# SBUF pools at multiples of 512 bytes, split weights 64 bytes into their tiles, in a hybrid decoder block

## The chip, the cores and the metric

One core of a Trainium2 chip runs the kernel. The metric is the device time of one execution in microseconds (us): the median of three timed executions before is 2871.86 (2871.25 to 2874.51). A further execution was recorded by the profiler. Engines are named as the profile names them: PE is TensorE, with PEld for its weight loads, DVE is VectorE, ACT is ScalarE, POOL is GpSimd, SP is SyncE, which issues the DMAs.

## The reference

One layer of a decoder block on a sequence of 512 tokens with 2,048 channels, all in float32: conditioning by `c`, an input projection, a gated short convolution and a gated linear recurrence (HGRN2) side by side, a merge, a SwiGLU network and three norms.

```python
def reference(x, c, w_ada, b_ada, norm_mix_g, w_in, conv_w, lb_param, gnorm_g,
              w_conv_out, w_hgrn_out, w_o, norm_ffn_g, w_ffn_gate, w_ffn_up, w_ffn_down,
              norm_final_g):
...
        h = rmsnorm(x, norm_mix_g[l]) * (1.0 + sc_m) + sh_m
        proj = h @ w_in[l]
        a_b, a_c, a_x, q, f_logit, i_in, g_out, gate_a, gate_b = jnp.split(proj, split_idx, axis=-1)

        y_a = (a_b * causal_depthwise_conv(a_c * a_x, conv_w[l])) @ w_conv_out[l]
...
        y_b = o.reshape(b, s, D_HGRN_V).astype(x.dtype) @ w_hgrn_out[l]

        merged = jax.nn.sigmoid(gate_a) * y_a + jax.nn.sigmoid(gate_b) * y_b
        x = x + gt_m * (merged @ w_o[l])

        h2 = rmsnorm(x, norm_ffn_g[l]) * (1.0 + sc_f) + sh_f
        ff = (jax.nn.silu(h2 @ w_ffn_gate[l]) * (h2 @ w_ffn_up[l])) @ w_ffn_down[l]
        x = x + gt_f * ff
```

## The kernel before

**Three products for one.** A float32 matrix product is made of three matmuls in the type float32r. Both operands are split: `hi` is the value rounded to float32r (a cast on ACT), `lo` is the rest (a subtraction on DVE). `mm3` (lines 218 to 225) and `m3` (618 to 621) issue weights-hi by activations-hi, weights-hi by activations-lo and weights-lo by activations-hi into one PSUM tile. Each matmul first loads a block of 128 x 128 weights, the stationary operand (LDWEIGHTS on PEld), and then streams the moving operand, 128 partitions by 256 or 512 columns of 4 bytes. The program has 17,316 float32r matmuls: 5,568 with 512 columns (lines 223 to 225, and 619 to 621 with a moving operand called hc) and 11,748 with 256 (all other of 619 to 621, some of 223 to 225, and lines 341 to 343). Plain float32 matmuls are few: 616, in the recurrence (lines 478 to 537) and in the sums of squares for the norms (289, 545, 918, 924), where a tile of ones is the weight.

**Operands change sides once.** In `v_block` (lines 334 to 343, 768 matmuls) the activations `h` are loaded as weights and the split weights `hi` and `lo` are the moving operand.

**Stages.** (1) 0 to 215 us: activations come in, the first modulation rows are reduced by DVE from 33.6 MB of `w_ada` (line 301), and the first projections run. (2) 215 to 772: the projections `q`, `f`, `g`, `v` and the convolution by `proj` and `v_block` with 512 columns, and the recurrence's small matmuls between them. (3) 772 to 1080: the gates, by one level of Strassen's scheme (`st_pass`, seven products of 256 columns in place of eight). (4) 1080 to 1390: the output projections with 512 columns, while DVE reduces the other modulation rows (`wm`, line 301), 67 MB of them over stages 2 and 4. (5) 1390 to 1465: the last of them with 256 columns. (6) 1465 to 2740: the SwiGLU network; Strassen passes for gate and up projections alternate with `down`, whose moving operand hc has 512 columns. (7) 2740 to 2868: the last down projection by halves of the tokens, the final norm, and the output.

**How weights arrive.** SP issues DMAs of 512 KB into `wr`, `ur` or `wm`. For each tile of weights ACT writes `hi` and DVE writes `lo`; in Strassen passes (`quad_s`, lines 663 to 670) DVE also forms four sums first. The pools of split weights are `wts` (stages 1 to 5, tiles of 4 x 256 or 8 x 128), `wts2` (stage 6, 7 x 128) and `tailw` (stage 7, 4 x 128). Weights are prepared two tiles ahead of their use (`next_w`, `next_g`, `next_u`). For two passes of stage 6 split weights are kept in the tiles `sb` of another pool (`kept`): 192 matmuls read them from there.

**Where tiles lie.** A pool is a range of each partition's SBUF bytes; pools are stacked from the left in the order in which they are opened, those with `side="right"` from the right end, and a pool opened later may stand where a closed one stood. In the built program of before, the first 16,384 bytes are scratch for DMA descriptors of software queues, small constants follow, and the pool `persist` lies from 16,512 to 22,496. From there on every pool on the left begins at 480 modulo 512, and so do the pools of activations on the right (`acto` at 196,576, `sacta` at 184,288), since tiles in them are multiples of 512 bytes. Slices of operands are steps of 512 or 1,024 bytes. So all 17,316 float32r matmuls have both weights and moving operand at 96 modulo 128 bytes. The tile of ones is at 0 modulo 128.

The order in which instructions stand on the engines is decided when the program is built, and is fixed then.

Of the kernel before, what the change touches and what calls it, by code (L numbers as in the profile page):

```python
# [8 lines left out]
F32 = mybir.dt.float32  # L9
F32R = mybir.dt.float32r  # L10
# [4 lines left out]
P = 128  # L15
# [26 lines left out]
RAMPS = (6,)  # L42
WFULL = 5
HCB = 5

COL_C = 0
COL_B = 16
# [14 lines left out]
def hybrid_block_kernel(ctx: ExitStack, tc: tile.TileContext, xt, cols, crow, wam, war, wst, win, wco, who, wo, wgt, wg, wu, wd,  # L62
                        cf, out):
    nc = tc.nc
    cnt = [0]

    def nm(s):
        cnt[0] += 1
        return f"{s}{cnt[0]}"

    pp = ctx.enter_context(tc.tile_pool(name="persist", bufs=1, reuse_waits="tile"))
    xpool = ctx.enter_context(tc.tile_pool(name="xact", bufs=8, reuse_waits="tile"))
    s1 = ctx.enter_context(ExitStack())
    r1 = ctx.enter_context(ExitStack())
# [6 lines left out]
    wp = s1.enter_context(tc.tile_pool(name="wts", bufs=3, reuse_waits="tile"))  # L81
# [35 lines left out]
    lbc = cp.tile([P, 64], F32, name="lbc")  # L117
    smat = cp.tile([P, 2, 4, P], F32, name="smat")
    epsc = pp.tile([P, 1], F32, name="epsc")
    ra = pp.tile([P, 2, T], F32, name="ra")  # L120
    rt = ra[:, 0, :]
    sums_ = {"t": ra[:, 1, :]}
# [8 lines left out]
    wlist = []  # L131
    wstate = {"dma": 0, "prep": 0, "use": 0, "raw": {}, "hl": {}}

    def w_pair(shape):
        return [wp.tile(list(shape), F32R, tag=t, name=nm(t)) for t in ("hi", "lo")]

    def w_dma():
        i = wstate["dma"]
# [8 lines left out]
    def w_prep():  # L147
        i = wstate["prep"]
        if i >= len(wlist):
            return  # L150
        while wstate["dma"] <= i:
            w_dma()
        raw = wstate["raw"].pop(i)
        hi, lo = w_pair((P, 4, 256))
        nw = wlist[i].shape[-1]
        S.copy(flat(hi)[:, 0:nw], raw[:, 0:nw])  # L156
        V.tensor_tensor(flat(lo)[:, 0:nw], raw[:, 0:nw], flat(hi)[:, 0:nw].bitcast(F32), op=ALU.subtract)  # L157
        wstate["hl"][i] = (hi, lo)
        wstate["prep"] = i + 1
# [503 lines left out]
    def quad_s(sm, raw, hi, lo):  # L663
        S.copy(hi[:, 0:3, :], raw[:, 1:4, :])  # L664
        V.tensor_tensor(sm[:, 0:2, :], raw[:, 1:3, :], raw[:, 0:1, :].to_broadcast([P, 2, P]), op=ALU.subtract)
        V.tensor_tensor(sm[:, 2, :], sm[:, 1, :], raw[:, 1, :], op=ALU.add)
        V.tensor_tensor(sm[:, 3, :], raw[:, 3, :], sm[:, 2, :], op=ALU.subtract)  # L667
        S.copy(hi[:, 3:7, :], sm)  # L668
        V.tensor_tensor(lo[:, 0:3, :], raw[:, 1:4, :], hi[:, 0:3, :].bitcast(F32), op=ALU.subtract)
        V.tensor_tensor(lo[:, 3:7, :], sm, hi[:, 3:7, :].bitcast(F32), op=ALU.subtract)  # L670
# [85 lines left out]
    def g_prep():  # L756
        i = gs["prep"]
        while gs["dma"] <= i:
            g_dma()
        _, _, u, strassen = glist[i]  # L760
        raw = gs["raw"].pop(i)[:, u, :, :]
        hi, lo = w_pair((P, 8, P))
        if strassen:
            quad_s(gs["sm"](), raw, hi, lo)
        else:
            quad_c(raw, hi, lo)
        gs["hl"][i] = (hi, lo)
        gs["prep"] = i + 1
# [196 lines left out]
    def u_dma():  # L965
        i = us["dma"]
        src = ulist[i][0] if i < tail0 else wd[(i - tail0) // 2, 10]
        raw = wr2.tile([P, 2, 4, P], F32, tag="raw", name=nm("ur"))
        nc.sync.dma_start(raw, src.rearrange("p (u b n) -> p u b n", u=2, b=4))
        if i < tail0:  # L970
            us["raw"][i] = us["raw"][i + 1] = raw
        else:
            for u in range(2):
                us["raw"][tail0 + torder.index(((i - tail0) // 2, u))] = raw
        us["dma"] = i + 2
# [64 lines left out]
    wp2 = s2.enter_context(tc.tile_pool(name="wts2", bufs=3, reuse_waits="tile"))  # L1040
    hcp = s2.enter_context(tc.tile_pool(name="hc", bufs=HCB, reuse_waits="tile"))
    tmp = s2.enter_context(tc.tile_pool(name="evt", bufs=1, reuse_waits="tile"))
# [10 lines left out]
    def u_prep():  # L1053
        i = us["prep"]
        while i not in us["raw"]:
            u_dma()
        _, u, kind = ulist[i]
        raw = us["raw"].pop(i)[:, u, :, :]
        pool = us["pool"] if kind == "T" else wp2
        shp = [P, 4, P] if kind == "T" else [P, 7, P]  # L1060
        if kind == "H":
            k = len(kept)
            t = sb[k // 2][k % 2]
            hi, lo = (t[:, 1 + 2 * b:3 + 2 * b, :].rearrange("p a (c n) -> p (a c) n", n=P) for b in range(2))
            kept.append((hi, lo))
        else:
            hi = pool.tile(shp, F32R, tag="hi", name=nm("uh"))
            lo = pool.tile(shp, F32R, tag="lo", name=nm("ul"))
        if kind == "S":
            quad_s(wp2.tile([P, 4, P], F32, tag="sm", name=nm("us"), bufs=2), raw, hi, lo)  # L1070
        else:
            with ExitStack() as order:
                for ins in us["after"] if i >= len(ulist) - 12 else ():
                    order.enter_context(tc.issue_after(ins.ins))
                S.copy(hi[:, 0:4, :], raw)  # L1075
                V.tensor_tensor(lo[:, 0:4, :], raw, hi[:, 0:4, :].bitcast(F32), op=ALU.subtract)  # L1076
        us["hl"][i] = (hi, lo)
        us["prep"] = i + 1

    def u_ahead(n=ULOOK):  # L1080
        i = us["use"]
        for k in range(i, min(i + n + 1, len(ulist))):
            if ulist[k][2] == "T" and us["pool"] is None:
                break
            if us["prep"] <= k:
                u_prep()
        while us["dma"] <= min(i + n + 3, len(ulist) - 2):
            u_dma()
# [305 lines left out]
```

## Time and profile before

| what | us |
|---|---|
| median of three timed executions | 2871.86 |
| the profiled execution's own time | 2870.43 |
| its span, first to last instruction | 2868.7 |
| PE busy | 2784.0 |
| DVE busy | 2237.1 |
| ACT busy | 1094.6 |

The span is what the profile covers; 1.7 us of the execution's time lie outside it. Busy time of PE counts a matmul from when it starts to wait for its columns to when its results are modelled to be out, so matmuls overlap in the records, and the distance of their starts tells more than their length. The mean granted TensorE clock is 0.992 of full speed; it is lower only at the start and at the end.

PE's own waits, as the profile groups them (what waited, for what, us in total, times, longest), add up to some 70 us; the five longest are:

```profile
PE m L225 <- DVE lo L157: 20.1, 19, 2.5
PE m L223 <- ACT hi L156: 14.6, 1, 14.6
PE x L289 <- DVE b L285: 8.6, 2, 8.1
PE m L343 <- DVE lo L157: 8.5, 4, 4.0
PE m L224 <- DVE o L208: 4.6, 1, 4.6
```

They lie in the first and fourth stage for the most part.

### The profile page before, as it was taken

The numbers are of one execution on the slowest core, as the hardware profiler recorded it, in microseconds if no ns is written. First come the engines' busy times: TensorE is split into PE (matmuls) and PEld (weight loads), VectorE is DVE, ScalarE is ACT, GpSimd is POOL, SyncE is SP. The second block draws the span as 40 slices with busy tenths as digits, with TensorE's granted clock in tenths as the row PEclk, the third lists the DMA queues.
The fourth block names the chain that finished last, engine by engine and source line by source line (L and its number), as shares of the span: only waits on it lengthen the run. The fifth ranks groups of instructions, "written<-read, shape, count | busy, mean of one in ns | idle before, by whom it ended". The sixth has DMA issues, their size and how long they took to land.

```text
span 2868.7 us, 46690 instructions
## 1 busy us (share of the span) xinstructions
PE 2784.0 (97%) x18524; PEld 2523.9 (88%) x18524; DVE 2237.1 (78%) x4326; ACT 1094.6 (38%) x1723; POOL 1.3 (0%) x7
## 2 busy tenths in 40 slices
PE   5999999999999999999999999999999999999997
PEld 3788888888899997787999899998999989899997
DVE  7998964738699986776689778696877869687786
ACT  4332423323244442222365343343433434343344
POOL 0000000000000000000000000000000000000000
PEclk8999999999999999999999999999999999999999
DMA  9865522322233458888643333333333333333332
GB/s 358 304 212 192 191 96 75 114 84 89 81 104 104 129 159 303 298 299 290 212 133 119 96 103 104 103 104 97 106 99 104 104 97 110 97 103 103 103 104 96
DMA packets 117616, 414.23 MB, mean 144 GB/s; under 512 B 12818, under 2 KB 17170, under 8 KB 117396
## 3 DMA queue, kind: packets, MB, share of 16 engines
q1 hardware_dynamic: 116244, 407.04, 43.3%
q10 hardware_dynamic: 1152, 4.19, 0.4%
q8 instruction: 145, 2.38, 0.3%
q14 instruction: 75, 0.61, 0.1%
HBM read 398.59 MB, written 12.59 MB: 143 GB/s over the span
## 4 chain that ended last, share of the span: by engine, by line
PE 81%; DVE 8%; DMA 8%; issue 2%; ACT 1%; SPq 0%; DVEq 0%; ACTq 0%
PE st L619 18%; PE st L620 18%; PE st L621 18%; PE m L223 6%; PE m L225 6%; PE m L224 6%; DMA wm<-in_war_dram 6%; DVE wm L301 2%; DVE o L301 2%; DVE lo L157 1%; PE m L621 1%; PE m L619 1%; PE m L620 1%; PE m L343 1%; PE m L341 1%
## 5 line engine op out<-in xcount | busy, mean ns | idle before, releaser
L621 PE MATMUL st<-sb,ul 128*128 128x256 f32 x1638 | 463.6, 283 | 0.0
L619 PE MATMUL st<-sb,uh 128*128 128x256 f32 x1638 | 463.5, 283 | 0.0
L620 PE MATMUL st<-sb,uh 128*128 128x256 f32 x1638 | 463.5, 283 | 0.0
L223 PE MATMUL m<-h,hi 128*128 128x512 f32 (+1 forms) x1152 | 433.9, 378 | 18.6 <-ACT hi L156 14.6
L225 PE MATMUL m<-h,lo 128*128 128x512 f32 (+1 forms) x1152 | 431.4, 375 | 13.4 <-DVE lo L157 13.1
L224 PE MATMUL m<-h,hi 128*128 128x512 f32 (+1 forms) x1152 | 429.8, 373 | 0.3 <-DVE h L328 0.2
L156 ACT CAST hi<-wr 128x1024 fp32r<-128x1024 f32 (+2 forms) x199 | 201.5, 1018 | 511.0 <-PE m L224 347.5
L664 ACT CAST uh<-ur 128x384 fp32r<-128x384 f32 x326 | 167.4, 513 | 435.4 <-PE st L620 254.3
L157 DVE TENSOR_TENSOR lo<-wr,hi 128x1024 fp32r<-128x1024 f32 (+2 forms) x199 | 234.9, 1183 | 113.2 <-ACT hi L156 111.9
L621 PEld LDWEIGHTS st<-sb,ul 128*128 128x128 f32 x1638 | 314.4, 192 | 0.5
L619 PEld LDWEIGHTS st<-sb,uh 128*128 128x128 f32 x1638 | 314.5, 192 | 0.4
L620 PEld LDWEIGHTS st<-sb,uh 128*128 128x128 f32 x1638 | 314.4, 192 | 0.0
L225 PEld LDWEIGHTS m<-h,lo 128*128 128x128 f32 x1152 | 217.7, 189 | 58.5 <-DVE lo L157 21.3
L223 PEld LDWEIGHTS m<-h,hi 128*128 128x128 f32 x1152 | 217.5, 189 | 58.2 <-ACT hi L156 15.7
L1076 DVE TENSOR_TENSOR ul<-ur,uh 128x512 fp32r<-128x512 f32 x210 | 143.6, 687 | 149.1 <-ACT uh L1075 148.8
L619 PE MATMUL st<-hc,uh 128*128 128x512 f32 (+1 forms) x656 | 255.9, 390 | 3.0 <-ACT hc L1235 2.0
L621 PE MATMUL st<-hc,ul 128*128 128x512 f32 (+1 forms) x656 | 252.7, 388 | 0.0
L1075 ACT CAST uh<-ur 128x512 fp32r<-128x512 f32 x210 | 129.6, 622 | 322.3 <-PE st L620 295.9
L224 PEld LDWEIGHTS m<-h,hi 128*128 128x128 f32 x1152 | 217.9, 189 | 38.6 <-DVE h L328 1.4
L620 PE MATMUL st<-hc,uh 128*128 128x512 f32 x648 | 251.6, 388 | 0.0
L670 DVE TENSOR_TENSOR ul<-us,uh 128x512 fp32r<-128x512 f32 x326 | 224.5, 689 | 1.7 <-ACT uh L668 1.6
L668 ACT CAST uh<-us 128x512 fp32r<-128x512 f32 x326 | 201.0, 617 | 17.7 <-DVE us L667 17.1
(306 smaller groups left out, 6262.0 us busy)
## 6 DMA issues: line engine op xcount, KB each, us to landing
wm<-in_war_dram SPq DMA_DIRECT2D x128, 512.0 KB, 4.5
wr<-in_win_dram SPq DMA_DIRECT2D x107, 512.0 KB, 3.6
ur<-in_wg_dram SPq DMA_DIRECT2D x96, 512.0 KB, 3.5
ur<-in_wu_dram SPq DMA_DIRECT2D x88, 512.0 KB, 3.5
ur<-in_wd_dram SPq DMA_DIRECT2D x88, 512.0 KB, 3.5
o<-in_wam_dram SPq DMA_DIRECT2D x64, 512.0 KB, 6.4
wr<-in_wgt_dram SPq DMA_DIRECT2D x60, 512.0 KB, 3.5
wr<-in_wo_dram SPq DMA_DIRECT2D x44, 512.0 KB, 4.3
```

Source lines behind the costliest of these rows:

```text
L156: S.copy(flat(hi)[:, 0:nw], raw[:, 0:nw])
L157: V.tensor_tensor(flat(lo)[:, 0:nw], raw[:, 0:nw], flat(hi)[:, 0:nw].bitcast(F32), op=ALU.subtract)
L223: TE.matmul(ps, wh, ah, start=first, stop=False)
L224: TE.matmul(ps, wh, al, start=False, stop=False)
L225: TE.matmul(ps, wl, ah, start=False, stop=last)
L619: TE.matmul(ps, wh, ah, start=first, stop=False, skip_group_check=True)
L620: TE.matmul(ps, wh, al, start=False, stop=False, skip_group_check=True)
L621: return TE.matmul(ps, wl, ah, start=False, stop=last, skip_group_check=True)
L664: S.copy(hi[:, 0:3, :], raw[:, 1:4, :])
L668: S.copy(hi[:, 3:7, :], sm)
L670: V.tensor_tensor(lo[:, 3:7, :], sm, hi[:, 3:7, :].bitcast(F32), op=ALU.subtract)
L1076: V.tensor_tensor(lo[:, 0:4, :], raw, hi[:, 0:4, :].bitcast(F32), op=ALU.subtract)
```

## The change

Tiles are moved within SBUF, and nothing else:

- The scratch for software DMA queues shrinks from 16,384 to 1,024 bytes.
- A tile of 8 columns (32 bytes) is added to `persist` and one of 120 columns (480 bytes) at the right end, so that the pools after them begin at multiples of 512 or of 256.
- A tile of split weights gets 32 columns more (`w_tile`), and the weights lie in it from column 16 on, that is from byte 64.

In the built program `persist` ends at 7,168 = 14 x 512, `acth` begins at 39,936 = 78 x 512, `acto` at 196,096 = 383 x 512. The places modulo 128 bytes, counted over the float32r matmuls of the program:

| moving operand at | weights at | before | after |
|---|---|---|---|
| 96 | 96 | 17,316 | 0 |
| 0 | 64 | 0 | 16,356 |
| 64 | 0 (lines 341 to 343) | 0 | 768 |
| 0 | 0 (weights kept in `sb`) | 0 | 192 |

The order of instructions on every engine, 23,968 rows in all, is row for row the same before and after; only line numbers and addresses differ.

```diff
+WOFF = 16
...
     pp = ctx.enter_context(tc.tile_pool(name="persist", bufs=1, reuse_waits="tile"))
+    padr = ctx.enter_context(tc.tile_pool(name="padr", bufs=1, side="right", reuse_waits="tile"))
+    padr.tile([P, 120], F32, name="padr")
...
     epsc = pp.tile([P, 1], F32, name="epsc")
+    pp.tile([P, 8], F32, name="padl")
     ra = pp.tile([P, 2, T], F32, name="ra")
...
+    def w_tile(pool, shape, tag, name):
+        a, b = shape[1:]
+        t = pool.tile([P, a * b + 32], F32R, tag=tag, name=nm(name))
+        return t[:, WOFF:WOFF + a * b].rearrange("p (a b) -> p a b", b=b)
+
     def w_pair(shape):
-        return [wp.tile(list(shape), F32R, tag=t, name=nm(t)) for t in ("hi", "lo")]
+        return [w_tile(wp, shape, t, t) for t in ("hi", "lo")]
...
-            hi = pool.tile(shp, F32R, tag="hi", name=nm("uh"))
-            lo = pool.tile(shp, F32R, tag="lo", name=nm("ul"))
+            hi = w_tile(pool, shp, "hi", "uh")
+            lo = w_tile(pool, shp, "lo", "ul")
...
-    nc = _bacc.Bacc("TRN2", target_bir_lowering=False, num_devices=1)
+    nc = _bacc.Bacc("TRN2", target_bir_lowering=False, num_devices=1, dynamic_dma_scratch_size=1024)
```

## The prediction

> **What bounds the kernel now.** I read the page first, busy time and the chain that ended last.
>
> ```profile
> PE 2784.0 (97%) x18524; PEld 2523.9 (88%) x18524; DVE 2237.1 (78%) x4326; ACT 1094.6 (38%) x1723; POOL 1.3 (0%) x7
> ...
> PE 81%; DVE 8%; DMA 8%; issue 2%; ACT 1%; SPq 0%; DVEq 0%; ACTq 0%
> ```
>
> TensorE (PE, its weight loads PEld) is the bound, so the cost of one matmul decides. Busy time by stage says where that holds (columns: window, its length, busy us and instructions of PE, PEld, DVE, ACT, POOL, then granted clock, DMA share, GB/s).
>
> ```profile
> 0.00:215.00 215.00, 174.85 (x794) 139.75 (x795) 191.20 (x311) 86.26 (x102) 1.33 (x7) 0.94 0.79 292
> 215.00:772.00 557.00, 551.56 (x3552) 462.71 (x3550) 376.89 (x528) 177.27 (x187) 0.00 (x0) 1.00 0.36 116
> 772.00:1080.00 308.00, 307.43 (x2549) 307.43 (x2550) 275.36 (x655) 146.14 (x268) 0.00 (x0) 0.99 0.39 126
> 1080.00:1390.00 310.00, 290.03 (x1249) 234.01 (x1248) 226.08 (x302) 70.58 (x70) 0.00 (x0) 0.99 0.85 292
> 1390.00:1465.00 75.00, 74.10 (x605) 73.46 (x604) 50.71 (x68) 43.56 (x59) 0.00 (x0) 1.00 0.47 148
> 1465.00:2740.00 1275.00, 1272.76 (x8882) 1195.22 (x8881) 1016.83 (x2249) 509.23 (x921) 0.00 (x0) 1.00 0.34 105
> 2740.00:2868.00 128.00, 113.28 (x903) 111.35 (x901) 100.03 (x220) 61.56 (x118) 0.00 (x0) 0.95 0.33 104
> ```
>
> Two stages move 292 GB/s and keep PE waiting (0 to 215 and 1080 to 1390 us); in the other five PE is full. There the spacing of the matmuls is the time. For 256 moving columns a stretch without any other form shows it, for 512 columns the timeline (start, length, instruction):
>
> ```profile
> 880.00:1060.00 180.00, 180.00 (x1503) 180.00 (x1502) 164.30 (x403) 85.44 (x162) 0.00 (x0) 1.00 0.39 123
> ```
>
> ```profile
> 1267.02 0.39 PE L223 MATMUL m<-o,hi 128*128 128x512 f32 x1
> ...
> 1267.25 0.39 PE L224 MATMUL m<-o,hi 128*128 128x512 f32 x1
> 1267.25 0.19 PEld L225 LDWEIGHTS m<-o,lo 128*128 128x128 f32 x1
> ...
> 1271.33 0.39 PE L224 MATMUL m<-h,hi 128*128 128x512 f32 x1
> ```
>
> Of the 1503, two to three straddle the edges (each record lasts 0.283 us), so 1500 start in 180.00 us: **120.0 ns** each. The last matmul quoted is the 19th after the first: 4.31 / 19 = **226.8 ns**. The difference over 256 columns gives 0.417 ns a column, and what is left, 120.0 - 106.8 = 13.2 ns, is 31.8 columns: **32 columns on every matmul, with 256 columns as with 512**. 32 float32 columns are 128 bytes of a partition. The weights for the next matmul start to load with the running one (1267.25).
>
> Plain float32 matmuls do not pay that. The chain has them in runs (start, us, what, count): 12 with 128 columns, 4 with 512, 8 with 256 (its first row here is one of its waits for a DMA, used below).
>
> ```profile
> 246.13 4.33 DMA wm<-in_war_dram
> ...
> 463.91 1.34 PE x L525 x12
> ...
> 757.17 1.72 PE x L545 x4
> ...
> 2834.22 1.73 PE x L924 x8
> ```
>
> 1.72 / 4 = 430 ns and 1.73 / 8 = 216.3 ns: 0.835 ns a column, two times 0.417, so each column is taken at half the rate; beyond that they leave 2.5 ns. The run of 12 takes 111.7 ns each, 5 ns over 128 x 0.835 = 106.9. That one is the weight load: it has 128 columns like all of them, and load records of 128 and 64 columns are 53 ns apart (191 and 138), 0.83 ns a column, so 106 ns of the load is columns.
>
> ```profile
> L525 PEld LDWEIGHTS x<-x,b 128*128 128x128 f32 x48 | 5.8, 191 | 0.9 <-ACT b L520 0.7
> L506 PEld LDWEIGHTS x<-x,x 128*64 128x64 f32 x64 | 4.0, 138 | 1.4 <-PE m L224 1.4
> ```
>
> Is it the load beside the matmul that costs the 32 columns? Here a load had to wait for VectorE (PEld at 1277.68), so that the matmul at 1276.09 ran with no load beside it:
>
> ```profile
> 1275.86 0.39 PE L223 MATMUL m<-h,hi 128*128 128x512 f32 x1
> 1275.87 0.19 PEld L224 LDWEIGHTS m<-h,hi 128*128 128x128 f32 x1
> 1276.09 0.39 PE L224 MATMUL m<-h,hi 128*128 128x512 f32 x1
> ...
> 1277.68 0.19 PEld L225 LDWEIGHTS m<-h,lo 128*128 128x128 f32 x1 [1.63 <-DVE lo L157]
> ```
>
> Its record is as long as that of its neighbour with a load, 0.39 us; without 13 ns it would read 0.38. Ends of matmuls are modelled, so this is weak, but it speaks for a cost of the matmul's own stream and not of two reads that collide.
>
> **The change part by part.** Every float32r matmul now reads its moving operand from a start at 96 modulo 128 bytes: 256 columns are 1,024 bytes, 8 pieces of 128 when they start at 0 and 9 when they start at 96; 512 columns 16 or 17. One piece more is 32 columns, which is the excess measured. Matmuls at half rate show none, as they would if a piece is fetched in the time of 32 full-rate columns and only the full-rate stream has no slack. That is my reading: **the excess is the ninth (seventeenth) piece, and it goes with a start at 0**. It is an inference: no float32r matmul of this trace starts elsewhere.
>
> What a matmul costs then: bounded below by its columns, 106.8 and 213.5 ns, above by today's 120.0 and 226.8. With 512 columns I take 213.5 + 2.5 (what float32 leaves) = 216.0: 10.8 ns saved. With 256 the weight load sets it, 111.7 as in the run of 12: 8.3 ns saved; 109.3 if the load can hide. The Trainium skill, "TensorE: Matmul & The Clock Gate", section "Wait — 56ns, not 53.3ns?", gives back-to-back matmuls their columns plus some 2.5 ns; the float32 runs agree with 2.5 ns, the float32r rows with 13.2 do not. By the page alone 256 columns would come to some 109 ns, and the sum would be 10,980 x 2.4 = 26 us deeper.
>
> Left out are the 768 matmuls of lines 341 to 343 (256 on each line, 192 of them from 215 to 772): there the split weight is the moving operand, at 64 after the change, still nine pieces. The counts by stage are those of one of three equal lines, L224 and L620:
>
> ```profile
> 0.00:215.00 215.00, 77.19 (x195) 37.42 (x196) 0.94 0.79 292
> 215.00:772.00 557.00, 235.93 (x605) 113.60 (x605) 1.00 0.36 116
> 1080.00:1390.00 310.00, 162.72 (x415) 78.50 (x416) 0.99 0.85 292
> 1390.00:1465.00 75.00, 54.72 (x193) 36.99 (x193) 1.00 0.47 148
> ```
>
> ```profile
> 772.00:1080.00 308.00, 241.00 (x850) 163.94 (x850) 0.99 0.39 126
> 1465.00:2740.00 1275.00, 905.62 (x2961) 565.62 (x2961) 1.00 0.34 105
> 2740.00:2868.00 128.00, 84.16 (x294) 57.00 (x293) 0.95 0.33 104
> ```
>
> - 215 to 772: 3 x 605 x 10.8 = 19.6 us. PE is 99% busy; the chain goes through waits for rows that come by DMA, like the one at 246.13, so I count 18.
> - 772 to 1080: 3 x 850 x 8.3 = 21.2. DVE's 275.4 us then stand in 287: 96%. I count 20.
> - 1390 to 1465: 3 x 193 x 8.3 = 4.8; I count 4.
> - 1465 to 2740: of 2961, 640 have 512 columns (line 620 on hc): 3 x 640 x 10.8 = 20.7, and 3 x 2321 x 8.3 = 57.8: 78.5. VectorE is near in its dense stretches:
>
> ```profile
> 1870.00:1948.00 78.00, 78.00 (x652) 78.00 (x651) 71.81 (x171) 36.28 (x68) 0.00 (x0) 1.00 0.33 105
> ```
>
>   78.0 x 111.7 / 120 = 72.6 us against 71.8 of DVE work: 99%. What covers the splitting today, PE's own time, is all but gone. I take off 0.8 us for each of ten such stretches: 70.
> - 2740 to 2868: 3 x 294 x 8.3 = 7.3, with waits: 5.
> - 0 to 215: 3 x 195 x 10.8 = 6.3, but DVE is busy 191 of 215: 1. 1080 to 1390: 3 x 415 x 10.8 = 13.4, but DMA is at 0.85: 2.
>
> Sum: 18 + 20 + 4 + 70 + 5 + 1 + 2 = **120 us**. The order of the instructions on every engine is unchanged, so nothing is moved past a queue. The padding adds no instruction. The scratch that gives up 15,360 bytes belongs to software queues, and the page lists hardware and instruction queues only: nothing. ScalarE and VectorE write the weights 64 bytes further; no row shows such a write, so I bound it by the gain above, which VectorE could eat, and take nothing.
>
> The profiled execution took 2870.43 us (span 2868.7), 1.4 below the median 2871.86; the forecast is **2752**. All seven products in full come to 152 us (2720), with 109.3 ns 26 more (2694).
>
> **The rivals.**
>
> *No change.* The 32 columns are a fixed cost of a float32r matmul. For it: every row quoted has the same start, so address and kind can't be parted, and float32 at a start of 96 pays nothing of it. Against: a fixed cost need not be 128 bytes to within a column. Time: 2872. The Trainium skill, same page, section "Step-by-step: what each phase is for", says that PE reads moving operand and weights through two independent ports and that a load takes no bandwidth from the running matmul. By that, 64 bytes between them change nothing, and only the start at 0 could; the row at 1276.09 agrees.
>
> *A collision of the two reads.* Weights and moving operand, both at 96 today, meet in the same 128 bytes, and the distance of 64 ends that. The price is the same 32 columns; lines 341 to 343 gain too (576 x 8.3 = 5 us): 2747. Against it stands 1276.09.
>
> *VectorE takes over.* It has 71.8 us of work in the 78 and sits idle there for ScalarE's half of each split (columns: busy us, mean ns, idle before).
>
> ```profile
> L669 DVE TENSOR_TENSOR ul<-ur,uh 128x384 fp32r<-128x384 f32 x30 | 16.6, 554 | 1.8 <-ACT uh L664 1.7
> ```
>
> Should the two add up to 75, 256 columns save 3 of 5.4 us: 45% of 21.2 + 57.8 is lost, 36 us: 2788.
>
> *Slower.* How load and matmul stand to each other does cost: after a restart one line's matmuls read 387 to 396 ns, where in steady flow all read 389.
>
> ```profile
> L223 PE MATMUL m<-h,hi x18: 387/389/396, 1278.0 to 1289.7; 128*128 128x512 f32 x18
> ```
>
> If the start at 0 saves nothing and the new distance of 64 puts all of them in the bad position, each pays 7 ns: 3 x 4,903 = 14,709 in the five PE-bound stages, 103 us: 2975. It decides once the spacing in the two pure stretches is above 120.0 and 226.8.
>
> **How the numbers follow.** Forecast 0.46 (own range 2694 to 2800), collision 0.10, VectorE 0.06, no change 0.26, slower 0.12. A measurement here tells 0.2% (6 us) from nothing. Faster 0.62, same 0.26, slower 0.12. The range takes in the deepest sum and the no-change case: 2694 to 2880.
>
> **What would show it.** The pure stretches: 111.7 and 216 ns a matmul confirm the step, 120.0 and 226.8 refute it. Lines 341 to 343 part the two causes: still at 120 if the start of the moving operand counts, faster if the distance does. So do the 192 matmuls whose weights are the kept tiles in sb (weights and moving operand both at 0): fast by the start, slow by the distance. DVE above 98% in 772 to 1080 would show it as the next bound. 1080 to 1390 should keep its length. I am wrong if spacing stays, or if VectorE's own instructions change their length.

## The result and the profile after

The change makes the kernel faster, by 50 us where 120 were forecast: median 2823.10 us (four runs, 2819.86 to 2825.55) against 2873.19 for the kernel before in the same session, ratio 0.9827, 95% interval 0.9813 to 0.9842. The profiled execution took 2819.86 us; its span is 2818.1, 50.6 less than before. Nine lines were added above the code, so that before's L619 to L621 are now L628 to L630, L223 to L225 are L232 to L234, and L341 to L343 are L350 to L352.

First the page of the changed kernel, busy time and the chain that ended last.

```profile
PE 2741.3 (97%) x18524; PEld 2455.2 (87%) x18524; DVE 2217.1 (79%) x4326; ACT 1099.7 (39%) x1723; POOL 1.3 (0%) x7
...
PE 80%; DMA 9%; DVE 8%; issue 2%; ACT 1%; SPq 0%; DVEq 0%; ACTq 0%
```

TensorE is as full as before. What changed is the price of a matmul, and it changed both ways. The pure stretch of 256 columns (same window and columns as in the prediction), and a stretch of 512 columns from the timeline:

```profile
880.00:1060.00 180.00, 180.00 (x1591) 180.00 (x1590) 171.24 (x421) 91.65 (x171) 0.00 (x0) 1.00 0.43 133
```

```profile
1261.77 0.40 PE L233 MATMUL m<-o,hi 128*128 128x512 f32 x1
1262.00 0.40 PE L234 MATMUL m<-o,lo 128*128 128x512 f32 x1
...
1267.60 0.39 PE L234 MATMUL m<-h,lo 128*128 128x512 f32 x1
1267.82 0.40 PE L232 MATMUL m<-h,hi 128*128 128x512 f32 x1
```

1591 records where there were 1503: less the two or three at the edges, 180.00 / 1588 = **113.3 ns** a matmul, down from 120.0. The last of the 512-column rows is the 26th after the first: 6.05 / 26 = **232.7 ns**, up from 226.8. VectorE, at 171 of 180 us, has not become the bound.

The stages show both. These rows of one line's instructions (count; duration in ns, least/median/most; first and last start) mark the gates, the start of the SwiGLU network and its end, before and then after.

```profile
L619 PE MATMUL st<-h,hi x464: 278/283/419, 772.6 to 1079.8; 128*128 128x256 f32 x155
L619 PE MATMUL m<-sa,uh x64: 278/283/469, 1461.3 to 1498.5; 128*128 128x256 f32 x64
```

```profile
L628 PE MATMUL st<-h,hi x464: 276/276/537, 781.6 to 1072.0; 128*128 128x256 f32 x155
L628 PE MATMUL m<-sa,uh x64: 276/276/469, 1450.5 to 1487.1; 128*128 128x256 f32 x64
```

| stretch | before | after | difference | forecast |
|---|---|---|---|---|
| start to first gate matmul (512 columns) | 772.6 | 781.6 | +9.0 | -19 |
| gates (256) | 307.2 | 290.4 | -16.8 | -20 |
| output projections (512, at the end 256) | 381.5 | 378.5 | -3.0 | -6 |
| SwiGLU to the end of the span (256 and 512) | 1407.4 | 1367.6 | -39.8 | -75 |

The gates did about what was forecast. The first stretch, nearly all 512 columns, went the wrong way.

Records are longer than the spacing by some 163 ns whatever the spacing (283 against 120.0 before, 276 against 113.3 here), so that in a steady flow the median length of a group tells its spacing: 276 is 113.3 ns, 281 some 118, 283 is 120, 389 is 226.7, 394 some 232. For the tables below, the spacing is the mean distance of the starts of neighbouring matmuls in the trace; in the kernels pauses are left out (over 135 ns with 256 columns, over 250 with 512).

### The profile page after: what moved, and what is told of

The parts are those of the page before. It is cut to its first block, busy times and chain, and to the rows that moved or that the text cites. A ratio compares the mean times of both kernels' runs of the same rounds, so it can differ in the third digit from the quotient of the medians.

```text
span 2818.1 us, 46688 instructions
## 1 busy us (share of the span) xinstructions
PE 2741.3 (97%) x18524; PEld 2455.2 (87%) x18524; DVE 2217.1 (79%) x4326; ACT 1099.7 (39%) x1723; POOL 1.3 (0%) x7
## 4 chain that ended last, share of the span: by engine, by line
PE 80%; DMA 9%; DVE 8%; issue 2%; ACT 1%; SPq 0%; DVEq 0%; ACTq 0%
PE st L628 18%; PE st L630 18%; PE st L629 18%; DMA wm<-in_war_dram 7%; PE m L232 7%; PE m L234 6%; PE m L233 6%; DVE wm L310 2%; DVE o L310 2%; DVE lo L166 1%; PE x L487 1%; PE m L630 1%; DMA modrow<-c_scratch 1%; PE m L352 1%; PE m L629 1%
## 5 line engine op out<-in xcount | busy, mean ns | idle before, releaser
L232 PE MATMUL m<-h,hi 128*128 128x512 f32 (+1 forms) x1152 | 438.3, 382 | 17.1 <-ACT hi L165 14.1
L630 PE MATMUL st<-sb,ul 128*128 128x256 f32 x1638 | 452.3, 276 | 0.3 <-DVE ul L679 0.3
L628 PE MATMUL st<-sb,uh 128*128 128x256 f32 x1638 | 452.2, 276 | 0.0
L629 PE MATMUL st<-sb,uh 128*128 128x256 f32 x1638 | 452.1, 276 | 0.0
L234 PE MATMUL m<-h,lo 128*128 128x512 f32 (+1 forms) x1152 | 436.1, 379 | 12.2 <-DVE lo L166 11.8
L166 DVE TENSOR_TENSOR lo<-wr,hi 128x1024 fp32r<-128x1024 f32 (+2 forms) x199 | 234.7, 1182 | 118.0 <-ACT hi L165 116.7
L630 PEld LDWEIGHTS st<-sb,ul 128*128 128x128 f32 x1638 | 307.5, 188 | 0.9 <-DVE ul L679 0.5
L628 PEld LDWEIGHTS st<-sb,uh 128*128 128x128 f32 x1638 | 307.5, 188 | 0.4
L629 PEld LDWEIGHTS st<-sb,uh 128*128 128x128 f32 x1638 | 307.5, 188 | 0.0
L234 PEld LDWEIGHTS m<-h,lo 128*128 128x128 f32 x1152 | 217.8, 189 | 61.5 <-DVE lo L166 19.0
L232 PEld LDWEIGHTS m<-h,hi 128*128 128x128 f32 x1152 | 217.6, 189 | 60.0 <-ACT hi L165 15.1
L628 PE MATMUL st<-hc,uh 128*128 128x512 f32 (+1 forms) x656 | 258.3, 394 | 2.9 <-ACT hc L1244 2.2
L630 PE MATMUL st<-hc,ul 128*128 128x512 f32 (+1 forms) x656 | 256.3, 393 | 0.0
```

Of the source, the lines that this page charges most:

```text
L232: TE.matmul(ps, wh, ah, start=first, stop=False)
L234: TE.matmul(ps, wl, ah, start=False, stop=last)
L628: TE.matmul(ps, wh, ah, start=first, stop=False, skip_group_check=True)
L629: TE.matmul(ps, wh, al, start=False, stop=False, skip_group_check=True)
L630: return TE.matmul(ps, wl, ah, start=False, stop=last, skip_group_check=True)
```

## The experiments

In these, *distance* is the weights' start less the moving operand's start, modulo 256 bytes. Before, it is 0 everywhere. In the changed kernel it is 64 or 192, since its tiles of split weights are 4,224, 3,712 or 2,176 bytes long, each 128 more than a multiple of 256 (only the 192 matmuls with kept weights stay at 0). Three values with slashes, as 64/64/192, are the distances of the three matmuls of one product: weights-hi twice, then weights-lo.

### Start or distance: two kernels and a bare measurement

`off0` keeps the aligned pools and takes the offset away; `start96` keeps the offset and moves the pools back.

```diff
off0:
-WOFF = 16
+WOFF = 0
start96:
-    padr.tile([P, 120], F32, name="padr")
+    padr.tile([P, 128], F32, name="padr")
...
-    pp.tile([P, 8], F32, name="padl")
+    pp.tile([P, 32], F32, name="padl")
```

> The kernel after with the split weights at byte 0 of their tiles again: pools at multiples of 512 bytes, so all 17,316 float32r matmuls have moving operand and weights both at 0 modulo 128 (distance 0, as before the change, but with an aligned start). Theory of the start (my prediction's): the gain is kept or grows, 256 columns at 113.3 ns or less, 512 columns at or below 226.7, time 2815 or less. Theory of the distance: nothing is left of it, 120.0 and 226.7 ns, time 2872 within 0.2% of before.

> The kernel after with other padding: pools begin at 96 modulo 128 again, weights stay 64 bytes into their tiles (moving operand at 96, weights at 32 modulo 128, distance 64). Theory of the start: the gain is gone, 120.0 and 226.7 ns, 2872. Theory of the distance: all of it stays, 113.3 ns for 256 columns, some 232 for 512, time 2823 like the kernel after.

`off0`: 2879.13 us, ratio 1.0019 (1.0009 to 1.0029): 6 us slower than before. `start96`: 2857.22, ratio 0.9946 (0.9931 to 0.9960): a third of the gain. Neither is as clean a test as its expectation took it for. In `off0` the tiles keep their 32 extra columns, so by the addresses of the built program its distance is 0 or 128, not 0 throughout. In `start96` the pools on the right come to lie 128 bytes from those on the left modulo 256, which swaps 64 and 192 for the moving operands there. What the pair shows: with the start at 0, 256 columns take 118.9 ns at distances of 0 and 128 and 113.4 at 64 and 192, so without the offset little is left of the gain; with the start left at 96, the offset alone brings them from 120.0 to 116.3. And both kernels run 512 columns at 232 ns, as the changed one does; in none of the three is their distance 0 throughout.

`spacing` measures the price alone: runs of 72 matmuls for each of 53 combinations of width, start and distance, first on a quiet core, then (`spacing_busy`) with VectorE and ScalarE at work beside them.

```python
for k in range(72): TE.matmul(ps[:, k % 2, 0:256], Z[:, 2064 + 128 * (k % 4):2192 + 128 * (k % 4)], Z[:, 512 * (k % 3):256 + 512 * (k % 3)], ...)  # distance 64
```

> No part of the block is computed: 53 groups of 72 float32r matmuls, a line each, on one tile, with no other engine at work. Distance of the weights from the moving operand 0 to 240 bytes in steps of 16, for 256 and 512 columns; starts of the moving operand at 32, 64 and 96; 320, 384 and 448 columns. Theory of the distance, with a stream that takes 17 periods for 16 columns: 113.3 ns for 256 columns at 64, 120.0 at 0, whatever the start; 512 columns at 226.7 where nothing collides, 320, 384 and 448 columns at 141.7, 170.0 and 198.3. Theory of a fixed cost of 16 periods a matmul: 320, 384, 448 columns at 140.0, 166.7, 193.3. If 512 columns are slower at 64 than at 0 here too, the loss there is the distance's; if both are at 226.7 it comes from the other engines or from distances that alternate.

> The same 53 groups while VectorE adds and ScalarE copies 1,024 columns without pause. If the other engines' reads and writes matter to the matmuls, groups that took the same before differ now, up to the 225 to 239 ns that 512 columns show in the kernel after; if not, every group keeps its spacing to within 1 ns.

The groups of the quiet run by line (mean ns of one record; L31 has 256 columns at distance 0, L35 at 64, L39 at 128; L47 has 512 columns at 0, L51 at 64, L55 at 128):

```profile
L31 PE MATMUL ps<-Z 128*128 128x256 f32 x72 | 8.8, 283 | 0.0
L35 PE MATMUL ps<-Z 128*128 128x256 f32 x72 | 8.3, 276 | 0.0
L39 PE MATMUL ps<-Z 128*128 128x256 f32 x72 | 8.7, 281 | 0.0
L47 PE MATMUL ps<-Z 128*128 128x512 f32 x72 | 16.5, 389 | 0.0
L51 PE MATMUL ps<-Z 128*128 128x512 f32 x72 | 17.0, 395 | 0.0
L55 PE MATMUL ps<-Z 128*128 128x512 f32 x72 | 17.0, 395 | 0.0
```

By the starts: 256 columns 119.9, 113.4 and 118.6 ns; 512 columns 227.2, 233.3 and 233.4. What is best for one width is bad for the other. With the busy engines each group came out the same to 0.1 ns, so other engines play no part in it, which leaves TensorE's own two reads. At starts of 32, 64 and 96 a distance of 0 gives the same 119.8 and 226.8 to 227.3, so the start by itself removes nothing at either width. At a distance of 64, though, these starts give 117.8 with 256 columns, where a start at 0 gave 113.4. The three widths between (320 columns 146.6 to 146.7 ns, 384 173.7 to 176.7, 448 202.2 to 206.6) came out by neither theory; `width`, below, returns to them.

### Each width at its own distance

`bywidth` puts the weights that meet 512 columns at distance 0 and those that meet 256 at 64, with tiles of a multiple of 512 bytes.

```diff
-    def w_tile(pool, shape, tag, name):
+    def w_tile(pool, shape, tag, name, off=WOFF, pad=128):
         a, b = shape[1:]
-        t = pool.tile([P, a * b + 32], F32R, tag=tag, name=nm(name))
-        return t[:, WOFF:WOFF + a * b].rearrange("p (a b) -> p a b", b=b)
+        t = pool.tile([P, a * b + pad], F32R, tag=tag, name=nm(name))
+        return t[:, off:off + a * b].rearrange("p (a b) -> p a b", b=b)
...
-        hi, lo = w_pair((P, 4, 256))
+        hi, lo = w_pair((P, 4, 256), WOFF if i in narrow else 0)
...
+            off, pad = 0 if kind == "D" else WOFF, 32 if kind == "T" else 128
+            hi = w_tile(pool, shp, "hi", "uh", off, pad)
+            lo = w_tile(pool, shp, "lo", "ul", off, pad)
```

> The kernel after, with the 64 bytes only for weights that meet 256 moving columns; weights that meet 512 columns lie at byte 0 of their tiles, and tiles of split weights are multiples of 512 bytes, so that all 5,568 matmuls with 512 columns have distance 0 modulo 256. Theory of the distance, read by width: 256 columns stay at 113.3 ns, 512 columns go back from some 232 to 226.7; 5.3 ns on the some 4,000 of them in stages that PE bounds is 21 us: 2802. Rival (the loss with 512 columns has another source, the aligned pools or the larger tiles): they stay at 232, 2823. Rival (another engine takes over): 512 columns at 226.7, but PE's waits grow by as much, 2823.

It missed: 2835.69 us (2830.82 to 2843.56), ratio 0.9876 (0.9856 to 0.9895), slower than the changed kernel. 512 columns were back at 227.3 ns, but 256 columns had risen to 116.3. One line's groups in its trace say where:

```profile
L634 PE MATMUL st<-sb,uh x1638: 275/281/303, 1515.9 to 2764.4; 128*128 128x256 f32 x182
L634 PE MATMUL st<-sa,uh x660: 275/281/282, 1515.2 to 2762.7; 128*128 128x256 f32 x165
...
L634 PE MATMUL st<-h,hi x464: 275/276/415, 771.6 to 1062.0; 128*128 128x256 f32 x155
L634 PE MATMUL st<-o,hi x224: 275/276/417, 772.4 to 1032.1; 128*128 128x256 f32 x112
```

The distance is 64 in all four rows, but the gates have 276 (113.3 ns) and the SwiGLU passes, each behind a run of 512 columns, mostly 281. Runs of matmuls hold one pace or the other: of 11,608 in long runs of 256 columns some 7,800 stand in runs that average 118 to 119 ns and some 3,800 in runs that average 113 to 114.

`spacing_fine`, with steps of 8 bytes and runs of 48, had the same in it.

> No part of the block is computed: 113 groups of 48 float32r matmuls, a line each, nothing else at work. 512 columns from a start at 0 with the weights 0 to 504 bytes away in steps of 8, 256 columns with 0 to 248; 512 columns at distance 8 from other starts; 256 columns at distance 64 from starts of 4 to 124. If distance acts through 64-byte halves of 128 bytes, spacing repeats every 128 bytes; if not, 512 columns at 256 will still be as fast as at 0 (226.7) and 128 slower (233). If start and distance act apart, 256 columns at distance 64 take 117.8 ns from every start that is no multiple of 128. A spacing below 113.3 or 226.7 ns anywhere would show that neither kernel is at the floor.

256 columns at distance 192, with the very addresses of `spacing`, read 117.8 ns where they had read 113.3, and 512 columns at distance 16 read 233.3 where they had read 226.7. The starts missed their expectation: at distance 64, 256 columns took 113.3 ns in the end from 16, 64 and 112, 116.7 from 28, 76 and 124, and 120 to 121 from 4, 40, 52, 88 and 100; the start at 64 had read 117.8 in `spacing`. At 512 columns no distance gives less than 226.7 ns: 0, 120, 256 and 376 reach it to 0.4 ns, most others lie between 230 and 234, and the pattern repeats after 256 bytes.

### Two paces, and what breaks the slow one

In the changed kernel the high and low parts of nearly all weights lie 128 bytes apart modulo 256, so within each triple of matmuls the distance switches: 64/64/192 in two thirds of the triples with 256 columns, 192/192/64 in the others, at 113.4 ns either way. In `bywidth` it stands at 64. `hilo` is `bywidth` with that switch put back, as 64/64/192.

```diff
     def w_tile(pool, shape, tag, name, off=WOFF, pad=128):
+        off = 3 * off if tag == "lo" and pad == 128 else off
```

> The weights that meet 512 columns stay at distance 0 modulo 256, as in bywidth; of those that meet 256 columns, the high part lies 64 bytes into its tile and the low part 192, as they stand in the changed kernel, where bywidth had both at 64. In bywidth's trace some 7,500 of 11,600 256-column matmuls ran at 117.8 ns and some 3,300 at 113.3, at the same distance of 64: the slow pace sets in behind a run of 512 columns and then holds. Theory that there are two paces for one distance and the matmul's past picks one, and that the switch between 64 and 192 at every low part breaks the slow one: 256 columns at 113.3 nearly everywhere, 512 columns at 226.7, so the changed kernel's 2823 less some 21 us, 2795 to 2810. Rival, that the 512-column work at distance 0 ahead of them sets the pace whatever the distances: 117.8 stays, 2830 to 2840.

> Only matmuls on float32r data, in place of the block: eight patterns of distance (256 columns at 64, at 192, at 64/64/192, at 192/192/64, at 0; 512 columns at 0, 64 and 64/64/192), 48 matmuls each, and each of them behind five different runs of 12 matmuls. Theory of two paces: at a constant distance of 64 or 192 the spacing is 113.3 behind some of the five and 117.8 behind others, the same for all 48; at 64/64/192 and 192/192/64 it is 113.3 behind all five; at 0 it is 120 behind all. 512 columns: 226.7 at 0, about 232 to 234 at the other two, behind all. Rival, that the distance alone sets the spacing: one value for each pattern, whatever ran ahead.

`hilo`: **2806.08 us**, ratio 0.9765 (0.9752 to 0.9779): the fastest kernel here, 66 us below the kernel before and 17 below the changed one. The row that read 281 in `bywidth` reads

```profile
L635 PE MATMUL st<-sb,uh x1638: 276/276/281, 1518.9 to 2739.4; 128*128 128x256 f32 x182
```

and 512 columns stayed at 227.3. In `lock` the same addresses took either pace, by what ran ahead (rows by line: L32 and L38 are 256 columns at distance 64, behind 512 columns at 0 and behind 256 columns at 128; L52 and L58 the same for the pattern 64/64/192):

```profile
L32 PE MATMUL ps<-Z 128*128 128x256 f32 x48 | 5.8, 281 | 0.0
L38 PE MATMUL ps<-Z 128*128 128x256 f32 x48 | 5.6, 276 | 0.0
L52 PE MATMUL ps<-Z 128*128 128x256 f32 x48 | 5.6, 276 | 0.0
L58 PE MATMUL ps<-Z 128*128 128x256 f32 x48 | 5.6, 276 | 0.0
```

| 256 columns, ns | behind 512 at 0 | 512 at 64 | 256 at 0 | 256 at 128 | 320 at 0 |
|---|---|---|---|---|---|
| distance 64 | 117.8 | 117.8 | 117.8 | 113.6 | 113.6 |
| 192 | 117.8 | 117.8 | 113.3 | 117.8 | 117.8 |
| 64/64/192 | 113.8 | 113.4 | 113.7 | 113.3 | 114.4 |
| 192/192/64 | 113.5 | 113.6 | 113.3 | 118.8 | 118.9 |
| 0 | 119.8 | 119.5 | 120.0 | 119.8 | 119.9 |

A sequence shows how it goes: at 64/64/192 behind 512 columns at 0 the spacings are 119, 117, 122, 116, 114, and then 113.3 for the rest. So the theory of two paces holds; that the switch always breaks the slow one doesn't, since 192/192/64 stayed slow behind two of the five. Behind 512 columns, the case of this kernel, it did not. The 512-column rows of `lock` did not depend on what ran ahead: 226.7 to 227.5 at 0, 233.3 to 233.4 at 64, 231.7 to 231.9 at 64/64/192. The two readings at distance 16 show that at other distances they can take either of two values as well.

### The start once more, and the excess by width

`hilo96` is `hilo` with the two paddings of `start96`.

> As hilo (256-column weights 64 and 192 bytes off their moving operand, 512-column weights at distance 0, or 128 for a seventh of them), but the two paddings that moved the pools are sized so that moving operands start at 96 modulo 128, as in the kernel before. Theory that a moving operand's start counts beside the distance at 256 columns (start96 ran them at 116.4 ns on average, paces between 113 and 120, with the same distances): 256 columns stay at 116 to 117 ns, the 512-column work is back near 227, so start96's 2857 less some 17 to 20 us, 2835 to 2845. Rival, that start96 was slow through its past (its 512-column work at 64 and 192) and the start is free: 256 columns at 113.3 and 2800 to 2812, as hilo.

2827.75 us, ratio 0.9849 (0.9836 to 0.9862), between the two expectations: 256 columns at 115.4 ns. But it is not the start alone that moved. As in `start96`, the pools on the right (moving operands `o`, `sx` and `sa`) come to lie 128 bytes from those on the left modulo 256. So 3,330 of the 256-column matmuls have distances of 192/192/64 in place of 64/64/192, and the 768 with 512 columns on `o` have 128 (232.5 ns). A row from the left (`sb`) and one from the right (`sa`):

```profile
L636 PE MATMUL st<-sb,uh x1638: 276/276/283, 1523.4 to 2756.6; 128*128 128x256 f32 x182
L636 PE MATMUL st<-sa,uh x660: 277/281/285, 1522.7 to 2754.8; 128*128 128x256 f32 x165
```

On the left, where the distances are those of `hilo`, 256 columns take 114.0 ns (`hilo`: 113.4); on the right 118.6 (`hilo`: 113.5). In `start96` the left has the distances of the changed kernel and takes 115.8 ns (there: 113.4). So the start counts beside the distance, by 0.6 to 2.4 ns where the distances stayed, and most of what `hilo96` loses lies where they changed with it. The pattern 192/192/64 alone does not explain that: from starts at 0 the changed kernel runs it at 113.3 ns, and `lock` at 118.8 behind two of its five runs. Whether the start or what ran ahead picks the pace is not shown.

`width` asks what is left at best.

> Only matmuls on float32r data, in place of the block: nine widths from 256 to 512 columns, each at distances 0, 64, 64/64/192, 88, 120, 168 and 192, 36 matmuls each, moving operand at 0. It asks what the least excess over the columns is (a column is 0.417 ns). Known: 16 columns at 256 (113.3 ns), 32 at 512 (226.7). Theory that it is a sixteenth of the columns: the least spacing is 141.7 ns at 320 columns, 170.0 at 384, 198.3 at 448. Rival, that it is one of two sizes, 16 or 32 columns, by how the two reads meet: 140.0 or 146.7 at 320, 166.7 or 173.3 at 384, 193.3 or 200.0 at 448.

| columns | 256 | 288 | 320 | 352 | 384 | 416 | 448 | 480 | 512 |
|---|---|---|---|---|---|---|---|---|---|
| least spacing of seven distances, ns | 113.3 | 131.3 | 145.3 | 159.9 | 173.4 | 186.7 | 200.0 | 216.0 | 226.7 |
| over the columns at 0.417 ns, in columns | 16 | 27 | 29 | 32 | 32 | 32 | 32 | 38 | 32 |

Neither expectation holds for all nine widths, and a sixteenth is out: from 352 columns on the least excess is mostly 32 columns; at 256 half of it goes.

### All kernels together

Spacings from the traces, with the 256-column matmuls of `v_block` and those with kept weights left out; the sum takes the prediction's counts for the five stages in which TensorE is full, 3 x (850 + 193 + 2321 + 294) - 192 = 10,782 matmuls with 256 columns (the 192 with kept weights did not change) and 3 x (605 + 640) = 3,735 with 512.

| kernel | 256 columns, ns | 512 columns, ns | by these, us | measured, us |
|---|---|---|---|---|
| before | 120.0 | 227.3 | | |
| after | 113.4 | 232.0 | -71 + 18 = -53 | -50 |
| off0 | 118.9 | 232.1 | -12 + 18 = +6 | +6 |
| start96 | 116.3 | 231.8 | -40 + 17 = -23 | -16 |
| bywidth | 116.3 | 227.3 | -40 + 0 = -40 | -38 |
| hilo | 113.5 | 227.3 | -70 + 0 = -70 | -66 |
| hilo96 | 115.4 | 228.1 | -50 + 3 = -47 | -44 |

Two numbers for each kernel carry the six differences, five of them to 4 us and `start96` to 7. Apart from that remainder nothing else that the change touches needs a term.

## Why the prediction was wrong

**The bound held.** TensorE is 97% busy before and after, and what it waits for is the same: the wait for `lo`, the longest group of before, now reads

```profile
PE m L234 <- DVE lo L166: 16.3, 16, 2.8
```

(us in total, times, longest; 20.1 before). VectorE did not take over: no group of its records got longer by more than 1 ns on average (the largest split in the SwiGLU network has a mean of 684 ns, before 689). It is busy for 92% of the gates and at most 98% of any 78 us (from 1488 us), and there TensorE is still busy for 76.7 of the 78. So the cover that the prediction feared to lose was still there.

**The step that failed** is "the excess is the ninth (seventeenth) piece, and it goes with a start at 0". Its own check refutes it: the matmuls whose weights are kept in sb have both operands at 0, and

```profile
L630 PE MATMUL m<-sa,sb x32: 278/283/386, 1464.2 to 1476.5; 128*128 128x256 f32 x32
```

their median is still 283, which is 120 ns. The other check agrees: lines 341 to 343, now 350 to 352, with moving operands at 64 and weights at 0, came down to 117.8 ns on average, at distances of 64 and 192. One of the three before and after:

```profile
L342 PE MATMUL m<-hi,h x256: 277/283/420, 61.1 to 663.0; 128*128 128x256 f32 x128
```

```profile
L351 PE MATMUL m<-hi,h x256: 276/281/415, 62.5 to 670.6; 128*128 128x256 f32 x128
```

What the runs showed in its place: the distance of weights and moving operand acts on the price of a matmul, and not the same way at both widths. In the bare loop, from distance 0 to 64, 256 columns went from 119.9 to 113.4 ns and 512 columns from 227.2 to 233.3. What ran ahead shifts this (`lock`), and so does the start at a distance of 64 (`spacing_fine`); a start at 0 by itself saves nothing.

**Behind it stands a reading of two points.** That both widths paid 32 columns was measured rightly; that one cause must then be behind both was not. At 512 columns none of the distances tried gives less than 226.7 ns: before was already at the best that any run here shows, and the change could only lose. At 256 columns 16 of the 32 can go. The trace of before could not tell, as all its matmuls had one start and one distance, and the prediction said so.

**By terms.** The forecast of 120 us is some 42 for 512 columns (18 + 20.7 + 1 + 2) and 78 for 256. Measured, 256 columns gave about 71, 6.6 ns each where 8.3 were expected: the weight load as the limit, 111.7 ns, was never reached. 512 columns cost about 18, 4.7 ns each where 10.8 were to be saved. The 512-column term is 60 of the 70 us of error. Two slips of the prediction's arithmetic change nothing in it: its seven products add up to 151 us, not 152, and 13.2 ns are 31.6 columns, not 31.8.

**The rivals.** *A collision of the two reads*, at a chance of 0.10, came nearest, since it let the distance count, but it expected 64 to be better at both widths and gave it the forecast's price (2747). What stood against it was the matmul without a load, 0.39 us like its neighbour. That record is shown to 10 ns, its end is modelled, and a change of 13 ns is hardly more; it should not have carried weight. By the Trainium skill, "TensorE: Matmul & The Clock Gate", section "Step-by-step: what each phase is for", a load takes no bandwidth from the running matmul. The runs do not bear this out for float32r data: in the bare loop, with nothing moved but the weights, from distance 0 to 64, the spacing changes by 6.5 ns at 256 columns and by 6.1 at 512. The 2.5 ns over the columns that the Trainium skill gives on the same page, section "Wait — 56ns, not 53.3ns?", were not seen with float32r either: the least was 113.3 - 106.8 = 6.5 ns. *Slower* was right for a third of the matmuls: a bad position at the new distance, priced at 7 ns, cost 512 columns 4.7. *No change* falls at both widths, *VectorE takes over* was not met.

What stays open: by what rule the two reads of TensorE meet. The runs give a table of spacings, repeating after 256 bytes of distance at 512 columns, and two paces at 256, but no mechanism that yields them. How much of the start's share is what ran ahead is open too. Whether a matmul without any load beside it runs faster was not tried.

## What to carry to other kernels

When an excess is read off two shapes, don't give it one cause until a third shape or address has been seen; here a bare loop of matmuls over widths and distances would have replaced the inference. Choose the distance between weights and moving operand for each width apart, and look at the spacing inside the kernel, not only in the loop: what runs ahead can leave the same addresses at another pace. Check what a padding does to the tiles behind the first: here it was the odd tile length that made high and low parts alternate, and that, not the offset alone, held the fast pace. And work out both addresses for every pool before calling a kernel a test of one of them: `off0` did not put all distances at 0, and `start96` and `hilo96` moved distances along with the start.

## What the runs showed of the hardware that was not expected

- At one pair of addresses a steady flow of 256-column float32r matmuls has two paces, 113.3 and 117.8 ns, each of which held to the end of a loop of 48 matmuls once it had set in (`lock`, L32 and L38). With 512 columns, distance 16 read 226.7 ns in one loop and 233.3 in another.
- Other engines' traffic leaves it alone: 53 groups agreed to 0.1 ns with VectorE and ScalarE idle and at work.
- The weight load's record shrank from 192 to 188 ns at 256 columns. It does not follow the spacing: in `spacing` it has a mean of 191.5 to 191.8 ns at distance 0 with 256 columns and of 187 to 190 in all other groups, among them ones with a spacing of 120.0 ns.
